# Two-part up products 512 columns wide in the last two feed-forwards, and unread identity products at three changes of stage

## The chip, the cores and the metric

The kernel runs on one core of one Trainium2 chip. The metric is the device time of one execution in microseconds, as the median of several runs. All data is float32.

## The reference, cut to what matters

Four residual layers work on 256 tokens of 1024 channels. Each has a token mixer (pooling in layers 0 and 3, stick-breaking attention in layer 1, a state-space layer in layer 2), a cross-attention to 256 memory tokens, and a gated feed-forward of 2816 channels. The feed-forward is what the change touches:

```python
def conv_glu_ffn(h, w_up, conv_w, conv_b, w_down):
    u = h @ w_up                                   # (256, 1024) @ (1024, 2 * 2816)
    u = sum(conv_w[CONV_WIDTH - 1 - k] * causal_shift(u, k) for k in range(CONV_WIDTH)) + conv_b
    val, gate = jnp.split(u, 2, axis=-1)
    return (jax.nn.silu(gate) * val) @ w_down      # (256, 2816) @ (2816, 1024)

for i in range(DEPTH):
    ...
    h = h + f          # f = conv_glu_ffn(rms_norm(h, ffn_norm_g[i]), ...)
return rms_norm(h, final_norm_g)
```

## The kernel before, in words

**Products in three parts.** Every operand of a large product is split into a rounded part (`hi`, type fp32r, a cast on ScalarE, line 70) and the rest (`lo`, a subtraction on VectorE, line 71). A product x·w is then three products on TensorE, which `mm3` issues (lines 65, 66, 67): hi·hi, the weights' hi with the activations' lo, and the weights' lo with the activations' hi. The product of the two rests is left out. Weights come from DRAM by the SP queue (line 88) into `raw` (three buffers), and are split in two halves into `whi` and `wlo` (six buffers in `wp`, three in the pool `fp` of the down projection).

**Norm and turn.** `norm_T` (line 200) is at the head of the attention mixer (`"mix"`), of the cross-attention (`"xa"`) and of the feed-forward (`"ffn"`). Token block 0 is normed, turned by TensorE against the identity (`turned`, line 223, eight transposes of 128x128) and split into `hi` and `lo` (`taken`); then block 1. `self.fill(...)` places work of other stages in between, such as parts of the next layer's K and V products. In the feed-forward of layer 0 that is the start of the state-space layer's preparation (`s5_start`), in those of layers 1 and 2 a part of a K product, in that of layer 3 nothing.

**The feed-forward.** `ffn` (line 1225) goes through 22 chunks `fc` of 128 channels, two to a load of weights (`f2`). A chunk has a value half (s = 0) and a gate half (s = 1). Each half sums eight pieces `c` of 128 input channels, of 256 token columns: 24 products a half, 48 a chunk, in one PSUM bank `u` of 512 columns. Behind them come, for each half, the convolution's middle tap and bias on ScalarE (line 1259) and its two other taps on VectorE (line 1261), both reading PSUM; then the SiLU (line 1263), the product of both halves (line 1264) and the split into `gg`. The down products (`flush`, 12 of 512 columns, into four banks `acc` that are kept through the stage) are issued two chunks later, through the list `pend`. At the end of the stage the last two chunks' down products follow, and `add_residual` adds the banks to `h` and sums the squares for the next norm (line 157).

**PSUM and order.** Four banks rotate for all products of the pool `psm`, four more are the `acc` banks. The order of instructions on each engine is made by a scheduler from the order of the code and the readiness that it expects; each engine then works in that order. `behind(...)` holds work back by hand.

Of the kernel before, what the change touches and what calls it, by code (L numbers as in the profile page):

```python
# [8 lines left out]
F32 = mybir.dt.float32  # L9
# [5 lines left out]
P = 128  # L15
T = 256
TT = T // P
D = 1024
DC = D // P
# [17 lines left out]
class Trunk:  # L37
# [152 lines left out]
    def norm_natural(self):  # L190
# [2 lines left out]
            self.normed(self.h, tt, xs[:, tt, :], self.ss[tt])  # L193
        return xs

    def transposed(self, xs, c, ps):
        for tt in range(TT):
            self.nc.tensor.transpose(ps[:, tt * P : (tt + 1) * P], xs[:, tt, c * P : (c + 1) * P], self.ident[:])

    def norm_T(self, which, l, where, scaled=True):  # L200

        nc = self.nc
        xs = self.big.tile([P, TT, D], F32, tag="xs", name="xs")
        g = xs[:, 1, :]
        nc.sync.dma_start(g, self.a[which + "_norm_g"][l].partition_broadcast(P))
        hi, lo = self.act_pair()
        self.fill(where + "0")
        halves = [slice(0, 512), slice(512, D)]

        def gained(tt):  # L210

            for s in halves:
                x = nc.vector.tensor_mul(xs[:, tt, s], self.h[:, tt, s], g[:, s])
            return x.ins

        def turned(tt):

            both = []
            for c4 in range(2):
                ps = self.bank() if tt else self.psa.tile([P, 512], F32, tag=f"acc{c4}", name="tp")  # L220
                for j in range(4):
                    c = 4 * c4 + j
                    nc.tensor.transpose(ps[:, j * P : (j + 1) * P], xs[:, tt, c * P : (c + 1) * P], self.ident[:])
                both.append(ps)
            return both

        def taken(tt, both):
            for c4 in range(2):
                f = lambda t: t[:, 4 * c4 : 4 * c4 + 4, tt * P : (tt + 1) * P]
                self.last = self.split(f(hi), f(lo), both[c4][:].rearrange("p (c t) -> p c t", c=4))  # L230

        if scaled:
            self.normed(self.h, 0, xs[:, 0, :], self.ss[0], g)
        else:
            gained(0)
        both = turned(0)

        if scaled:
            r = self.rstd(self.ss[1])
            first = self.squared, self.scaled  # L240
        else:
            first = gained(1),
        with self.behind(*first):
            taken(0, both)
        self.fill(where)
        if scaled:
            gained(1)
            nc.vector.tensor_scalar_mul(xs[:, 1, halves[0]], xs[:, 1, halves[0]], r[:, 0:1])
            nc.scalar.mul(xs[:, 1, halves[1]], xs[:, 1, halves[1]], r[:, 0:1])
        both = turned(1)  # L250
        self.fill(where + "1")
        taken(1, both)
        self.after = [(), self.last, self.last]
        self.transposed_all = (*self.last, self.powed)
        return hi, lo
# [968 lines left out]

    def ffn(self, l, fp):
        nc = self.nc
        hi, lo = self.norm_T("ffn", l, "fnorm")
        up = self.a["ffn_w_up"][l].rearrange("(c p) (s n) -> p c s n", p=P, s=2)
        down = self.a["ffn_w_down"][l].rearrange("(c p) n -> p c n", p=P)
        accs = self.accs()  # L1230
        pend = []

        ug = self.acts.tile([P, 8, T], F32, tag="ah", name="ug")
        gg = self.acts.tile([P, 8, T], F32R, tag="al", name="gg")

        def flush():
            fc, gh, gl, w, k = pend.pop(0)
            for tt in range(TT):
                s = slice(tt * P, (tt + 1) * P)
                for nh in range(2):  # L1240
                    self.mm3(accs[2 * nh + tt][:], (gh[:, s], gl[:, s]), w(k, slice(512 * nh, 512 * (nh + 1))), fc == 0, fc == FC - 1)

        for f2 in range(FC // 2):
            wu = [self.load(up[:, :, s, T * f2 : T * (f2 + 1)], DC, T) for s in range(2)]
            wd = self.load(down[:, 2 * f2 : 2 * f2 + 2, :], 2, D, fp)
            for j in range(2):
                fc = 2 * f2 + j
                self.fill(f"up{fc}")
                ps = self.bank("u")
                u = ug[:, 2 * (fc % 3) : 2 * (fc % 3) + 2, :]  # L1250
                for s in range(2):
                    out = ps[:, s * T : (s + 1) * T]
                    for c in range(DC):
                        self.mm3(out, wu[s](c, slice(j * P, (j + 1) * P)), (hi[:, c, :], lo[:, c, :]), c == 0, c == DC - 1)
                for s in (1, 0):
                    out = ps[:, s * T : (s + 1) * T]
                    col = s * FC + fc
                    cw = [self.cwT[:, l, k, col : col + 1] for k in range(4)]
                    nc.scalar.activation(u[:, s, :], out, AF.Identity, bias=cw[3], scale=cw[2])  # L1259
                    for sh in (1, 2):  # L1260
                        nc.vector.scalar_tensor_tensor(u[:, s, sh:], out[:, : T - sh], cw[2 - sh], u[:, s, sh:], ALU.mult, ALU.add)  # L1261
                g = ug[:, 6 + fc % 2, :]
                nc.scalar.activation(g, u[:, 1, :], AF.Silu)
                nc.vector.tensor_mul(g, g, u[:, 0, :])
                gh, gl = gg[:, 2 * (fc % 4), :], gg[:, 2 * (fc % 4) + 1, :]
                last = self.split(gh, gl, g)
                pend.append((fc, gh, gl, wd, j))
                if len(pend) > 2:
                    flush()

        self.after = [(), last, last]
        while pend:
            flush()
        for nh in range(2):
            for tt in range(TT):
                self.add_residual(nh, tt, accs[2 * nh + tt])
# [145 lines left out]
```

## Time and profile before

| | us |
|---|---|
| median of 3 runs | 1481.85 |
| lowest, highest | 1478.66, 1484.84 |
| profiled execution, its time | 1482.43 |
| profiled execution, span from the first to the last instruction | 1480.7 |
| TensorE busy in the span | 1426.4 |
| VectorE busy | 1096.5 |
| ScalarE busy | 839.3 |
| mean granted TensorE clock, share of full speed | 0.982 |

Times in rows of the trace count from the span's start. The up products of a feed-forward are the rows `u<-ah,whi`, `u<-al,whi` and `u<-ah,wlo`; the down products are `acc<-whi,gg` and `acc<-wlo,gg`; the transposes of `norm_T` are `tp<-ident,xs` for token block 0 and `mm<-ident,xs` for block 1. Engines are PE (TensorE), PEld (its weight loads), DVE (VectorE), ACT (ScalarE), POOL (GpSimd) and SP. In a row of the order in time, the first column is the start in us, the second the length, and brackets hold the idle time before it and what ended it. In a sum over a stretch stand the stretch and its length, then for each engine the busy time and the number of instructions, then the granted clock, the busy share of the DMA engines and GB/s.

### The profile page before, as it was taken

The numbers are of one execution on the slowest core, as the hardware profiler recorded it, in microseconds if no ns is written. First come the engines' busy times: TensorE is split into PE (matmuls) and PEld (weight loads), VectorE is DVE, ScalarE is ACT, GpSimd is POOL, SyncE is SP. The second block draws the span as 40 slices with busy tenths as digits, with TensorE's granted clock in tenths as the row PEclk, the third lists the DMA queues.
The fourth block names the chain that finished last, engine by engine and source line by source line (L and its number), as shares of the span: only waits on it lengthen the run. The fifth ranks groups of instructions, "written<-read, shape, count | busy, mean of one in ns | idle before, by whom it ended". The sixth has DMA issues, their size and how long they took to land.

```text
span 1480.7 us, 25386 instructions
## 1 busy us (share of the span) xinstructions
PE 1426.4 (96%) x10354; PEld 1316.4 (89%) x10354; DVE 1096.5 (74%) x1722; ACT 839.3 (57%) x1351; POOL 124.3 (8%) x128
## 2 busy tenths in 40 slices
PE   7999999998999999999997789999999999999997
PEld 7897999998998989999987668999999999899996
DVE  6969888767886577978783857678677776677675
ACT  7654655547895455645453256565555565565553
POOL 3401000000000000111103500000000030000000
PEclk9999999999999999999998989999999999999999
DMA  7667656645444545776758675455555563465551
GB/s 261 229 164 220 222 199 206 219 135 166 151 149 161 187 148 191 250 225 221 235 192 234 238 233 170 158 171 199 183 187 182 178 210 136 143 220 171 189 181 43
DMA packets 205681, 279.74 MB, mean 189 GB/s; under 512 B 23740, under 2 KB 163132, under 8 KB 203644
## 3 DMA queue, kind: packets, MB, share of 16 engines
q1 hardware_dynamic: 198556, 260.46, 53.0%
q0 software_dynamic: 6432, 17.13, 3.5%
q8 instruction: 81, 1.33, 0.4%
q10 hardware_dynamic: 576, 0.52, 0.1%
q14 instruction: 36, 0.29, 0.1%
HBM read 264.24 MB, written 16.94 MB: 190 GB/s over the span
## 4 chain that ended last, share of the span: by engine, by line
PE 79%; DVE 9%; DMA 6%; ACT 3%; issue 1%; POOL 0%; SPq 0%; DVEq 0%; POOLq 0%; ACTq 0%
PE u L66 10%; PE u L67 10%; PE u L65 10%; PE mm L66 7%; PE mm L65 7%; PE mm L67 7%; PE acc L65 7%; PE acc L66 7%; PE acc L67 7%; DMA raw<-in_ffn_w_up_dram 3%; DVE wlo L71 2%; DMA raw<-in_xa_wkv_dram 2%; ACT whi L70 1%; DVE ug L1261 1%; DMA raw<-in_s_w_glu_dram 1%
## 5 line engine op out<-in xcount | busy, mean ns | idle before, releaser
L71 DVE TENSOR_TENSOR wlo<-raw,whi 128x1024 fp32r<-128x1024 f32 x430 | 519.3, 1220 | 157.0 <-ACT whi L70 148.4
L70 ACT CAST whi<-raw 128x1024 fp32r<-128x1024 f32 (+1 forms) x450 | 460.1, 1045 | 198.8 <-DMA raw<-in_ffn_w_up_dram 55.3
L65 PE MATMUL u<-ah,whi 128*128 128x256 f32 x1408 | 400.6, 285 | 1.7 <-DVE ug L1261 1.3
L66 PE MATMUL u<-al,whi 128*128 128x256 f32 x1408 | 399.8, 284 | 0.4 <-DVE al L71 0.4
L67 PE MATMUL u<-ah,wlo 128*128 128x256 f32 x1408 | 399.5, 284 | 0.0
L65 PEld LDWEIGHTS u<-ah,whi 128*128 128x128 f32 x1408 | 271.2, 193 | 6.3 <-issue 2.5
L66 PEld LDWEIGHTS u<-al,whi 128*128 128x128 f32 x1408 | 271.2, 193 | 3.4 <-DVE al L71 0.9
L67 PEld LDWEIGHTS u<-ah,wlo 128*128 128x128 f32 x1408 | 271.2, 193 | 0.0
L1261 DVE SCALAR_TENSOR_TENSOR ug<-u,cwT,ug 128x255 f32<-128x255 f32 x352 | 168.5, 480 | 101.3 <-ACT ug L1259 96.2
L1259 ACT ACTIVATE ug<-u,cwT 128x256 f32<-128x256 f32 x176 | 99.0, 563 | 185.6 <-PE u L67 125.0
L65 PE MATMUL acc<-whi,gg 128*128 128x512 f32 x352 | 138.0, 392 | 0.0
L66 PE MATMUL acc<-wlo,gg 128*128 128x512 f32 x352 | 137.9, 392 | 0.0
L67 PE MATMUL acc<-whi,gg 128*128 128x512 f32 x352 | 136.9, 389 | 0.0
L66 PE MATMUL mm<-al,whi 128*128 128x256 f32 x384 | 109.9, 286 | 0.1
L65 PE MATMUL mm<-ah,whi 128*128 128x256 f32 x384 | 109.8, 286 | 0.0
L67 PE MATMUL mm<-ah,wlo 128*128 128x256 f32 x384 | 109.4, 285 | 0.0
L176 POOL TENSOR_TENSOR r<-v,mhalf 128x1 f32<-128x1 f32 x28 | 22.7, 813 | 810.5 <-DVE v L172 678.7
L67 PEld LDWEIGHTS acc<-whi,gg 128*128 128x128 f32 x352 | 66.1, 188 | 14.4
L65 PEld LDWEIGHTS acc<-whi,gg 128*128 128x128 f32 x352 | 66.4, 189 | 11.7
L66 PEld LDWEIGHTS acc<-wlo,gg 128*128 128x128 f32 x352 | 66.4, 189 | 10.7
L66 PEld LDWEIGHTS mm<-al,whi 128*128 128x128 f32 x384 | 74.6, 194 | 0.8 <-DVE al L71 0.6
L65 PEld LDWEIGHTS mm<-ah,whi 128*128 128x128 f32 x384 | 74.6, 194 | 0.3 <-ACT ah L70 0.2
(355 smaller groups left out, 2564.9 us busy)
## 6 DMA issues: line engine op xcount, KB each, us to landing
raw<-in_ffn_w_up_dram SPq DMA_DIRECT2D x88, 1024.0 KB
raw<-in_ffn_w_down_dram SPq DMA_DIRECT2D x44, 1024.0 KB
raw<-in_xa_wkv_dram SPq DMA_DIRECT2D x30, 1024.0 KB
raw<-in_xa_wq_dram SPq DMA_DIRECT2D x16, 1024.0 KB
raw<-in_xa_wo_dram SPq DMA_DIRECT2D x16, 1024.0 KB
raw<-in_sb_w_qkv_dram SPq DMA_DIRECT2D x12, 1024.0 KB
raw<-in_s_w_glu_dram SPq DMA_DIRECT2D x8, 1024.0 KB
raw<-in_sb_w_o_dram SPq DMA_DIRECT2D x4, 1024.0 KB
```

What stands on the lines that cost most here:

```text
L65: mm(out, lh, rh, start=start, stop=False)
L66: mm(out, lh, rl, start=False, stop=False)
L67: self.multiplied = mm(out, ll, rh, start=False, stop=stop).ins
L70: x = self.nc.scalar.copy(hi, src)
L71: y = (eng or self.nc.vector).tensor_sub(lo, src, hi.bitcast(F32))
L176: self.powed = nc.gpsimd.tensor_tensor(r[:], v[:], self.mhalf[:], ALU.pow).ins
L1259: nc.scalar.activation(u[:, s, :], out, AF.Identity, bias=cw[3], scale=cw[2])
L1261: nc.vector.scalar_tensor_tensor(u[:, s, sh:], out[:, : T - sh], cw[2 - sh], u[:, s, sh:], ALU.mult, ALU.add)
```

## The change

In the feed-forwards of layers 2 and 3 (`wide`), the activations' two parts lie side by side: four pieces in one tile, four in the other, each piece 256 columns of `hi` and then 256 of `lo`. The weights' hi part multiplies all 512 columns in one product; the weights' lo part multiplies the 256 columns of `hi`, into the right half of the same bank. A half of a chunk then fills one bank, a chunk two. The two columns' halves of a bank are put together by a copy on ScalarE and an addition on VectorE, into `sums` in SBUF, and the convolution's steps read that instead of PSUM, the value half first instead of the gate half.

Apart from that, `turn_over` issues products of the identity with itself (full precision, 256 columns) into a bank that nothing reads: six before the first transposes of layer 1's attention, and five behind the first transposes of the feed-forwards of layers 0 and 3.

```diff
+    def turn_over(self, n):
+        ps = self.bank("idle")
+        for _ in range(n):
+            self.nc.tensor.matmul(ps[:, :T], self.ident[:], self.ident[:].unsqueeze(1).to_broadcast([P, 2, P]), start=True, stop=True)
...
-    def norm_T(self, which, l, where, scaled=True):
+    def norm_T(self, which, l, where, scaled=True, wide=False):
...
-        hi, lo = self.act_pair()
+        if wide:
+            hi, lo = self.act_pair(4, 2 * T)
+        else:
+            hi, lo = self.act_pair()
...
         def taken(tt, both):
             for c4 in range(2):
                 f = lambda t: t[:, 4 * c4 : 4 * c4 + 4, tt * P : (tt + 1) * P]
-                self.last = self.split(f(hi), f(lo), both[c4][:].rearrange("p (c t) -> p c t", c=4))
+                to = [(hi, lo)[c4][:, :, n + tt * P : n + (tt + 1) * P] for n in (0, T)] if wide else (f(hi), f(lo))
+                self.last = self.split(*to, both[c4][:].rearrange("p (c t) -> p c t", c=4))
...
+        if (l, which) == (1, "mix"):
+            self.turn_over(6)
         both = turned(0)
+        if (l, which) in ((0, "ffn"), (3, "ffn")):
+            self.turn_over(5)
...
     def ffn(self, l, fp):
-        hi, lo = self.norm_T("ffn", l, "fnorm")
+        wide = l > 1
+        hi, lo = self.norm_T("ffn", l, "fnorm", wide=wide)
...
+        sums = self.kv.tile([P, 2, 2, T], F32, tag="vh", name="sums") if wide else None
+
+        def up_wide(out, w, j):
+            for c in range(DC):
+                x = (hi, lo)[c // 4][:, c % 4, :]
+                wh, wl = w(c, slice(j * P, (j + 1) * P))
+                nc.tensor.matmul(out, wh, x, start=c == 0, stop=False, skip_group_check=True)
+                nc.tensor.matmul(out[:, T:], wl, x[:, 0:T], start=False, stop=c == DC - 1, skip_group_check=True)
...
-                ps = self.bank("u")
...
+                if wide:
+                    both = [self.bank("u"), self.bank("u")]
+                    for s in range(2):
+                        up_wide(both[s][:], wu[s], j)
+                else:
+                    ps = self.bank("u")
...
-                for s in (1, 0):
-                    out = ps[:, s * T : (s + 1) * T]
+                for s in range(2) if wide else (1, 0):
+                    if wide:
+                        out = sums[:, fc % 2, s, :]
+                        nc.scalar.copy(out, both[s][:, T:])
+                        nc.vector.tensor_add(out, out, both[s][:, 0:T])
+                    else:
+                        out = ps[:, s * T : (s + 1) * T]
```

More of the change, by code (lines that the diff above doesn't have):

```diff
@@ L1248, in ffn @@
                 self.fill(f"up{fc}")
-                ps = self.bank("u")
                 u = ug[:, 2 * (fc % 3) : 2 * (fc % 3) + 2, :]
-                for s in range(2):
-                    out = ps[:, s * T : (s + 1) * T]
-                    for c in range(DC):
-                        self.mm3(out, wu[s](c, slice(j * P, (j + 1) * P)), (hi[:, c, :], lo[:, c, :]), c == 0, c == DC - 1)
-                for s in (1, 0):
-                    out = ps[:, s * T : (s + 1) * T]
+                if wide:
[4 more added lines that the diff above has]
+                    ps = self.bank("u")
+                    for s in range(2):
+                        out = ps[:, s * T : (s + 1) * T]
+                        for c in range(DC):
+                            self.mm3(out, wu[s](c, slice(j * P, (j + 1) * P)), (hi[:, c, :], lo[:, c, :]), c == 0, c == DC - 1)
+                for s in range(2) if wide else (1, 0):
[4 more added lines that the diff above has]
+                    else:
+                        out = ps[:, s * T : (s + 1) * T]
                     col = s * FC + fc
```

## The prediction, made before the kernel was run

> **What bounds the kernel now.** I read the page first: busy shares, the clock row, the chain.
>
> ```profile
> PE 1426.4 (96%) x10354; PEld 1316.4 (89%) x10354; DVE 1096.5 (74%) x1722; ACT 839.3 (57%) x1351; POOL 124.3 (8%) x128
> ...
> PEclk9999999999999999999998989999999999999999
> ...
> PE 79%; DVE 9%; DMA 6%; ACT 3%; issue 1%; POOL 0%; SPq 0%; DVEq 0%; POOLq 0%; ACTq 0%
> ```
>
> TensorE carries the time: busy 96% of the span, 79% of the chain. VectorE, at 74%, is next. Since a busy TensorE need not be a fast one, I went to the sums over stretches: layer 3's feed-forward, and in it one pass of 17.00 us (two of the 22 chunks).
>
> ```profile
> core 0: us, PE busy (x) PEld busy (x) DVE busy (x) ACT busy (x) POOL busy (x), PEclk, DMA share, GB/s
> 1284.00:1472.00 188.00, 188.00 (x1317) 176.97 (x1316) 134.01 (x200) 104.51 (x156) 0.00 (x0) 0.99 0.49 166
> 1360.02:1377.02 17.00, 17.00 (x122) 16.02 (x121) 12.27 (x19) 9.55 (x14) 0.00 (x0) 1.00 0.55 187
> ```
>
> TensorE has no idle time there, at full clock, while VectorE has 4.73 us of 17.00 free, ScalarE 7.45, and the DMA engines work 0.55 of the time. A chunk takes 8.50 us. The order in time on TensorE says what it is made of (first column is the start):
>
> ```profile
> 1304.98 0.28 PE L65 MATMUL u<-ah,whi 128*128 128x256 f32 x1
> ...
> 1310.62 0.28 PE L67 MATMUL u<-ah,wlo 128*128 128x256 f32 x1
> 1310.73 0.40 PE L65 MATMUL acc<-whi,gg 128*128 128x512 f32 x1
> ...
> 1313.26 0.39 PE L67 MATMUL acc<-whi,gg 128*128 128x512 f32 x1
> 1313.48 0.28 PE L65 MATMUL u<-ah,whi 128*128 128x256 f32 x1
> ```
>
> From 1304.98 to 1310.73 stand the 48 up products of a chunk (2 halves, 8 pieces, 3 products): 5.75 us, 0.120 apart. From 1310.73 to 1313.48 stand 12 down products of 512 columns: 2.75 us, 0.229 apart. The durations in the rows (0.28, 0.40) overlap, so I reckon with distances. Two products of 256 columns take 0.240, one of 512 takes 0.229: some 0.011 us goes with the product, not with its columns.
>
> **The change part by part.** *Wide products.* For each of 2 layers x 22 chunks x 2 halves x 8 pieces = 704 places, three products of 256 columns (0.360) become one of 512 and one of 256 (0.229 + 0.120 = 0.349). TensorE is the bound throughout these stages, so all of it is on the path: 704 x 0.011 = 7.7 us. Bounds: none (0) if the short product behind the long one costs more than in a row of its own kind, and 704 x 0.020 = 14 us with the last long product's 0.22 (1313.26 to 1313.48) for all of them. I take 8.0, near the mean of 12 and a little towards that shorter one. Weight loads fall from three to two a place and lie beside the products as before.
>
> The Trainium skill, "TensorE: Matmul & The Clock Gate", section "Wait — 56ns, not 53.3ns?", puts a warm product's fixed part at some 2.5 ns; by that the sum would be 704 x 2.5 ns = 1.8 us instead of 8.0. The rows above differ, and the measurement decides.
>
> *The conversions behind it.* Per half ScalarE copies 256 columns out of PSUM and VectorE adds 256. Nearest rows of 256 columns:
>
> ```profile
> L71 DVE TENSOR_TENSOR gg<-ug,gg 128x256 fp32r<-128x256 f32 x88 | 36.8, 418 | 4.0 <-ACT gg L70 3.8
> L1263 ACT ACTIVATE ug<-ug 128x256 f32<-128x256 f32 x88 | 35.8, 407 | 0.0
> L70 ACT CAST gg<-ug 128x256 fp32r<-128x256 f32 x88 | 35.7, 406 | 51.4 <-DVE ug L1264 51.3
> ```
>
> VectorE's chunk grows from 12.27 / 2 = 6.14 by 2 x 0.42 to 6.97 us, ScalarE's from 4.78 by 2 x 0.41 to 5.59; a chunk of TensorE shrinks from 8.50 to 8.50 - 16 x 0.0114 = 8.32. So VectorE is at 84%, and I cost this at nothing. Cover: a chunk's down products are issued only after the up products of the chunk two later (the list `pend`), some 14 us. Where the cover is shortest is the last chunk: its down products come 24 products (5.5 us) behind its up products, and its conversions now run like this:
>
> ```profile
> 1463.94 0.56 ACT L1259 ACTIVATE ug<-u,cwT 128x256 f32<-128x256 f32 x1 [4.30 <-PE u L67]
> 1464.53 1.00 DVE L1261 SCALAR_TENSOR_TENSOR ug<-u,cwT,ug 128x255 f32<-128x255 f32 x2 [3.71 <-ACT ug L1259]
> ...
> 1468.17 0.42 DVE L71 TENSOR_TENSOR gg<-ug,gg 128x256 fp32r<-128x256 f32 x1 [0.47 <-ACT gg L70]
> ```
>
> That is 4.65 us from 1463.94 to 1468.59. With two banks, the value half is complete 2.8 us earlier and its steps no longer stand in this row; the gate half keeps copy, add, activation with its hand-over (0.59), two steps (1.00) and the gate's four of about 0.45: 4.3 us. Still inside 5.5. The chunk uses two of four banks instead of one; the next but one needs them again 14 us later, hidden likewise. The sums lie in the place of the cross-attention's V, which the next layer takes again long after; no DMA is added or moved. In the queues of ScalarE and VectorE the conversions of the next weights stand behind the new steps, and TensorE waits for those. If that cover goes, every us of VectorE over 8.32 in a chunk shows 44 times.
>
> *The first product of the stage.* It now needs both parts of its piece, not only the cast one. Layer 3's change of stage on TensorE:
>
> ```profile
> 1278.38 1.03 PE L223 MATMUL tp<-ident,xs 128*128 128x128 f32 x8
> 1281.58 1.06 PE L223 MATMUL mm<-ident,xs 128*128 128x128 f32 x8 [2.17 <-issue]
> 1282.88 0.51 PE L65 MATMUL u<-ah,whi 128*128 128x256 f32 x2 [0.24 <-ACT ah L70]
> 1283.61 0.39 PE L66 MATMUL u<-al,whi 128*128 128x256 f32 x1 [0.22 <-DVE al L71]
> ```
>
> Only the product at 1282.88 ran before VectorE's part was there at 1283.6; to lose that head start costs 0.12 to 0.2 in each of two layers: +0.3 in all.
>
> *Identity products.* A drop of the clock is read from TensorE's work in equal steps of 3.41 us and the clock in the next one:
>
> ```profile
> 140.44:143.85 3.41, 3.19 (x13) 2.90 (x14) 3.41 (x5) 3.41 (x5) 0.00 (x0) 0.50 0.74 267
> 335.00:338.41 3.41, 1.06 (x8) 0.86 (x8) 2.95 (x6) 2.79 (x11) 1.29 (x2) 1.00 0.09 13
> 338.41:341.83 3.42, 3.16 (x12) 2.58 (x13) 2.63 (x5) 2.71 (x5) 0.00 (x0) 0.50 0.84 292
> 341.83:345.24 3.41, 3.41 (x18) 3.41 (x17) 1.74 (x3) 3.40 (x4) 0.00 (x0) 0.50 0.04 11
> 809.45:812.87 3.42, 2.12 (x24) 1.73 (x16) 2.57 (x5) 1.84 (x5) 3.42 (x5) 1.00 0.74 260
> 812.87:816.28 3.41, 3.37 (x15) 2.80 (x16) 2.83 (x4) 3.38 (x4) 3.39 (x5) 1.00 0.90 322
> 1280.49:1283.91 3.42, 1.87 (x12) 1.46 (x13) 2.73 (x5) 2.88 (x5) 0.46 (x1) 1.00 0.00 0
> 1283.91:1287.32 3.41, 3.41 (x18) 3.41 (x17) 3.26 (x4) 3.41 (x5) 0.00 (x0) 0.50 0.00 0
> ```
>
> 1.06 and 1.87 us of work were followed by half clock, 2.12 was not. A step at half clock holds 18 products at its edges, so some 16 whole ones, 0.213 each; at 0.120 they take 1.92, so a full step at full clock is worth 1.49 us.
>
> What does one identity product cost? It is of full-precision operands; the nearest row with such operands and no transposing is
>
> ```profile
> 844.53 1.95 PE L1080 MATMUL acc<-tu,v 128*32 128x128 f32 x64
> ```
>
> By the code these are 32 products in four column groups, two records each. If the groups run side by side, 16 records follow each other at 0.12 for 128 columns; so 0.23 for 256, and 0.46 for a product's two. If not, 0.03 each, 0.12 for a product. I take 0.46, since it fills the wait: five are 2.3 us, six 2.8.
>
> Layer 3: five start at 1279.4 and end at 1281.7, where the next transposes start at 1281.58: delay 0.1. The step 1280.49 then holds 1.87 + 1.2 us, above 2.12: clock kept, -1.5 + 0.1 = -1.4. Bounds 0 and -1.9 (half of 3.7 us). Layer 0: the half-clock step holds 13 products, at most 13 x 0.093 = 1.2 us; I take -1.0, since some waits are in it; bounds 0 and -1.2. They also push the state-space transposes behind them back on TensorE and with them ScalarE's copies; covered by products that need the second half of the pieces only later. Layer 1's attention:
>
> ```profile
> 336.89 1.06 PE L223 MATMUL tp<-ident,xs 128*128 128x128 f32 x8 [3.02 <-DVE v L172]
> 338.52 1.97 PE L223 MATMUL mm<-ident,xs 128*128 128x128 f32 x8 [0.57 <-DVE xs L248]
> 340.31 0.58 PE L65 MATMUL mm<-ah,whi 128*128 128x256 f32 x1
> 341.04 0.58 PE L66 MATMUL mm<-al,whi 128*128 128x256 f32 x1
> ```
>
> Six fit the wait of 3.02, so the transposes do not slip and step 335.00 holds 1.06 + 1.4. But step 338.41 then holds 1.06 of transposes, two single products and a run from about 340.5 or 341: close to 2.1, undecided. Both steps at full clock: 4.20 us from 341.04 to 345.24 become 2.36, and the transposes' 1.97 become 1.06, of which 0.5 is kept: -2.4. Only the first: about -0.9. And if the order on TensorE puts them into an earlier wait, between the last down products, they cost up to 6 x 0.46 = +2.8. I take -1.2.
>
> *Sum.* -8.0 + 0.3 - 1.4 - 1.0 - 1.2 = -11.3. The profiled execution took 1482.4 (its span 1480.7 and 1.7 around it), 0.6 above the median of 1481.85: 1481.9 - 11.3 = 1470.6, say **1470.5**.
>
> **The rivals.** *A, the forecast*: 1470.5; own range 1466 to 1474.4, from -15.5 (9.5 for the wide part, all three clocks kept with 2.4 + 1.9 + 1.2) to -7.4.
>
> *B, the clocks fall as before or the fillers cost what they bring*: only the wide part stays, 1481.9 - 7.7 = 1474.2, with one delay 1477. For: the step of 3.41 us runs free of the kernel, and a shift of a few us moves the idle time to other steps. Against: 2.12 sufficed. The Trainium skill, same page, "Part 4: PE-mode transpose", says that transposes do not count as work for the clock; by it the three steps would still fall, and the time would be B's. The row 809.45, where 16 of 24 records are transposes and the clock stayed, speaks against it.
>
> *C, slower: VectorE and ScalarE become the bound by handing over.* In order, a half now goes ScalarE, VectorE, ScalarE, VectorE. If no weight conversion stands in the waits of VectorE, a chunk costs it 6.97 + 2 x 0.59 (two activations) + 0.41 (gate) + 0.47 (cast) = 9.0; 44 x (9.0 - 8.50) = +22, less 3.6 of the clocks: 1500. It decides from 8.50 + 3.6 / 44 = 8.6 a chunk. For: 84% busy in order. Against: a pass has 4.73 us free, of which the adds take 1.7, and its conversions of weights can stand in these waits. *C2*, a chunk between 8.4 and 8.5: 1474.4 to 1480.
>
> *D, the pair costs as much as the three*, the fixed part being that of the long one's weight change: only the clocks, 1481.9 - 3.6 + 0.3 = 1478.6.
>
> **How the numbers follow.** A 0.58, B 0.18, C 0.06, C2 0.11, D 0.07. Half a per cent is 7.4 us, about what a measurement here can tell from no change. Faster (under 1474.4): A and half of B, 0.67. Slower (over 1489): C, 0.06. Same: 0.27. Range 1464.5 to 1479: below A's end for steps of the clock that fall elsewhere (one is 1.5 us), up to D, leaving out C and the ends of C2 and A.
>
> **What would show it.** Right: in layers 2 and 3 a chunk of 8.3 us, up products 0.35 a pair, TensorE still without idle time, VectorE near 84%; full clock in the steps after the three changes; 16 identity products of about 0.46 inside the old waits. Wrong: TensorE waiting for `gg` or `wlo` in those layers; pairs at 0.36; identity products between down products; half clock behind them.

## The result, and the profile after

The changed kernel takes 1471.79 us (median of 4 runs, 1471.04 to 1473.01) against 1480.53 for the kernel before beside it (1478.66 to 1484.84): ratio 0.9946, 95% interval 0.9924 to 0.9967, a gain of 8.7 us. The prediction of 1470.5 is 1.3 us below that. The profiled execution of the change took 1471.25, its span 1469.5, 11.2 us less than the span of before.

From the page of the changed kernel, the busy times, the clock in 40 slices and the chain by engine:

```profile
PE 1420.6 (97%) x9682; PEld 1279.3 (87%) x9682; DVE 1122.0 (76%) x1810; ACT 866.2 (59%) x1439; POOL 124.4 (8%) x128
...
PEclk9999999999999999999999999999999999999999
...
PE 75%; DVE 11%; DMA 7%; ACT 3%; issue 2%; POOL 0%; SPq 0%; DVEq 0%; POOLq 0%; ACTq 0%
```

TensorE issues 672 records less (704 fewer in the wide products, 32 more for the 16 identity products), VectorE and ScalarE 88 more each. TensorE is still the bound. The two slices with an 8 in the clock row of before are gone, but they lie in the state-space layer (777 to 814 and 851 to 888 us), where the change has no instruction. Sum over a stretch of the changed kernel inside layer 2's feed-forward (layer 3's is alike):

```profile
1000.00:1140.00 140.00, 140.00 (x738) 119.45 (x737) 114.12 (x188) 90.67 (x154) 0.00 (x0) 1.00 0.56 188
```

No idle time on TensorE, full clock. A chunk takes 8.386 us, and of that VectorE works 114.12 / 140 x 8.386 = 6.84, or 82%. The order in time on TensorE in layer 3:

```profile
1321.07 0.39 PE L1260 MATMUL u<-ah,whi 128*128 128x512 f32 x1
1321.30 0.28 PE L1261 MATMUL u<-ah,wlo 128*128 128x256 f32 x1
1321.41 0.40 PE L1260 MATMUL u<-ah,whi 128*128 128x512 f32 x1
...
1326.71 0.40 PE L65 MATMUL acc<-whi,gg 128*128 128x512 f32 x1
...
1329.46 0.39 PE L1260 MATMUL u<-ah,whi 128*128 128x512 f32 x1
```

Sixteen pairs stand from 1321.07 to 1326.71: 5.64 us, 0.3525 a pair. The down products take 2.75 as before. So a chunk went from 8.50 to 8.39, where 8.32 was expected.

The changes of stage, in the order of time on TensorE of the changed kernel (layer 0, layer 1's attention, layer 3):

```profile
135.92 2.32 PE L200 MATMUL idle<-ident 128*128 128x256 f32 x10
...
333.24 2.75 PE L200 MATMUL idle<-ident 128*128 128x256 f32 x12
336.42 1.06 PE L233 MATMUL tp<-ident,xs 128*128 128x128 f32 x8 [0.43 <-DVE v L172]
338.05 1.43 PE L233 MATMUL mm<-ident,xs 128*128 128x128 f32 x8 [0.57 <-DVE xs L263]
...
1270.88 1.03 PE L233 MATMUL tp<-ident,xs 128*128 128x128 f32 x8
1271.75 2.32 PE L200 MATMUL idle<-ident 128*128 128x256 f32 x10
1274.09 1.06 PE L233 MATMUL mm<-ident,xs 128*128 128x128 f32 x8
1276.11 0.50 PE L1260 MATMUL u<-ah,whi 128*128 128x512 f32 x1 [0.96 <-DVE ah L71]
```

Five identity products take 2.32, six 2.75: 0.46 each. They stand in the waits of before; what is left of layer 1's wait is 0.43 of 3.02, and layer 3's second transposes follow the first by 3.21, before by 3.20. The clock behind them, as sums over stretches of the length of a clock step:

```profile
141.00:144.41 3.41, 2.90 (x22) 2.69 (x23) 3.41 (x5) 3.41 (x5) 0.18 (x1) 1.00 0.77 293
339.38:342.79 3.41, 3.07 (x24) 2.87 (x24) 1.65 (x3) 3.24 (x4) 0.00 (x0) 1.00 0.52 179
1276.11:1279.52 3.41, 3.41 (x19) 2.99 (x20) 3.27 (x4) 3.41 (x5) 0.00 (x0) 1.00 0.03 5
```

All three at full clock, where before all three places showed 0.50.

The starts of the same instructions in both traces, after minus before, give the account of the two profiled executions (a chunk's term in the prediction is 8.0 / 44 = 0.18):

| place | change in time, us | predicted |
|---|---|---|
| start-up | +0.6 | - |
| layer 0's feed-forward, head | -1.1 | -1.0 |
| layer 1's attention | -2.3 | -1.2 |
| layer 1's feed-forward and the state-space layer, to 889.00 of before | -2.2 | - |
| layer 2's feed-forward, head and first three chunks | -0.3 | -0.4 |
| layer 2's next 18 chunks | -2.0 | -3.3 |
| from there to layer 3's first transposes, one chunk with it | -0.1 | -0.2 |
| layer 3's feed-forward, head and first three chunks | -1.6 | -1.8 |
| layer 3's next 18 chunks | -2.0 | -3.3 |
| end, one chunk with it | -0.1 | -0.2 |

What the head of layer 3 costs and gains can be taken apart with the kernel that has the identity products alone (in the experiments below). From the second transposes to the first up product behind the first down products it has the rows 1276.70 and 1298.60, the changed kernel 1274.09 and 1295.91:

```profile
1276.70 1.06 PE L233 MATMUL mm<-ident,xs 128*128 128x128 f32 x8
...
1298.60 0.28 PE L65 MATMUL u<-ah,whi 128*128 128x256 f32 x1
```

```profile
1295.91 0.39 PE L1260 MATMUL u<-ah,whi 128*128 128x512 f32 x1
```

Before it is 23.40 us (1281.58 to 1304.98), with the identity products alone 21.90, with the whole change 21.82. So the clock gives 1.5 there. The wide products give 0.08 more, three chunks of 0.113 less 0.26 for the later start.

The -2.2 ahead of layer 2 was in no term. In the trace of before two steps there ran at half clock; the same work in the changed kernel ran at full clock. That gave 2.75; a step at half clock late in layer 1's feed-forward (759.22) and other waits took 0.5 back. First before, then after:

```profile
874.30:877.72 3.42, 2.52 (x6) 2.04 (x7) 3.31 (x4) 2.98 (x3) 0.00 (x0) 0.50 0.66 235
877.72:881.13 3.41, 3.41 (x9) 2.64 (x9) 0.00 (x0) 0.00 (x0) 0.00 (x0) 0.50 0.73 161
```

```profile
869.50:883.99 14.49, 13.04 (x61) 10.59 (x60) 8.73 (x9) 9.39 (x10) 0.00 (x0) 1.00 0.63 206
```

The change has no instruction there, and where the waits of this stretch fall among the steps differs between traces: the kernel with the wide products alone, with the same order of instructions up to here, is 5.9 us behind before's trace at 797.78 and 0.5 behind it at 883.10. Without this stretch and the start-up, the places that the change touches gave 9.5 of the 11.2 us; the medians differ by 8.7.

### The profile page after: what moved, and what is told of

Same layout as the page of the kernel before. It is cut to its first block, busy times and chain, and to the rows that moved or that the text cites. A ratio compares the mean times of both kernels' runs of the same rounds, so it can differ in the third digit from the quotient of the medians.

```text
span 1469.5 us, 24256 instructions
## 1 busy us (share of the span) xinstructions
PE 1420.6 (97%) x9682; PEld 1279.3 (87%) x9682; DVE 1122.0 (76%) x1810; ACT 866.2 (59%) x1439; POOL 124.4 (8%) x128
## 4 chain that ended last, share of the span: by engine, by line
PE 75%; DVE 11%; DMA 7%; ACT 3%; issue 2%; POOL 0%; SPq 0%; DVEq 0%; POOLq 0%; ACTq 0%
PE u L1260 11%; PE mm L66 7%; PE mm L65 7%; PE mm L67 7%; PE acc L65 7%; PE acc L66 7%; PE acc L67 7%; PE u L1261 6%; PE u L66 4%; PE u L65 4%; PE u L67 4%; DMA raw<-in_ffn_w_up_dram 3%; DVE wlo L71 3%; DMA raw<-in_xa_wkv_dram 2%; ACT whi L70 2%
## 5 line engine op out<-in xcount | busy, mean ns | idle before, releaser
L65 PE MATMUL u<-ah,whi 128*128 128x256 f32 x704 | 200.9, 286 | 2.4 <-DVE ug L1298 2.0
L66 PE MATMUL u<-al,whi 128*128 128x256 f32 x704 | 199.9, 284 | 0.5 <-DVE al L71 0.5
L67 PE MATMUL u<-ah,wlo 128*128 128x256 f32 x704 | 199.8, 284 | 0.0
L65 PEld LDWEIGHTS u<-ah,whi 128*128 128x128 f32 x704 | 135.6, 193 | 5.3 <-issue 3.4
L66 PEld LDWEIGHTS u<-al,whi 128*128 128x128 f32 x704 | 135.7, 193 | 1.7 <-DVE al L71 0.7
L67 PEld LDWEIGHTS u<-ah,wlo 128*128 128x128 f32 x704 | 135.7, 193 | 0.0
L1260 PE MATMUL u<-ah,whi 128*128 128x512 f32 x352 | 128.3, 398 | 1.0 <-DVE ah L71 1.0
L1260 PE MATMUL u<-al,whi 128*128 128x512 f32 x352 | 128.2, 398 | 0.0
L1298 DVE SCALAR_TENSOR_TENSOR ug<-sums,cwT,ug 128x255 f32<-128x255 f32 (+1 forms) x176 | 84.4, 481 | 37.4 <-ACT ug L1296 35.3
L1261 PE MATMUL u<-ah,wlo 128*128 128x256 f32 x352 | 98.9, 281 | 0.0
L1261 PE MATMUL u<-al,wlo 128*128 128x256 f32 x352 | 98.7, 281 | 0.0
```

The source lines that it names most:

```text
L65: mm(out, lh, rh, start=start, stop=False)
L66: mm(out, lh, rl, start=False, stop=False)
L67: self.multiplied = mm(out, ll, rh, start=False, stop=stop).ins
L1260: nc.tensor.matmul(out, wh, x, start=c == 0, stop=False, skip_group_check=True)
L1261: nc.tensor.matmul(out[:, T:], wl, x[:, 0:T], start=False, stop=c == DC - 1, skip_group_check=True)
```

## The experiments

Ratios are to the kernel before, run beside each; its medians there were 1481.28, 1480.51 and 1480.73, single runs between 1475 and 1487.

**Each half of the change alone.**

```diff
-        if (l, which) == (1, "mix"):
-            self.turn_over(6)
-        if (l, which) in ((0, "ffn"), (3, "ffn")):
-            self.turn_over(5)
```

> The change without its identity products. Theory 1 (the parts add up, each by its own rows): the wide products alone give 44 chunks x 0.114 us = 5.0 us, less 0.6 at the two stage heads, so a ratio to before of about 0.997; chunks of 8.39 us in layers 2 and 3; half clock returns in the steps after the change of stage in layer 0's feed-forward, layer 1's attention and layer 3's feed-forward. Rival (the clock was kept by something else, the earlier start of work): no half clock there and a ratio of 0.9945 as with the whole change.

Without identity products: 1480.03 us, ratio 0.999 (0.9975 to 1.0004). The three places are at half clock again, sums over stretches:

```profile
143.56:146.97 3.41, 3.41 (x18) 3.41 (x18) 3.41 (x4) 3.41 (x5) 0.00 (x0) 0.50 0.40 143
...
341.53:344.94 3.41, 2.97 (x14) 2.40 (x13) 2.16 (x4) 2.66 (x5) 0.00 (x0) 0.50 0.70 243
...
1280.20:1283.61 3.41, 2.76 (x11) 2.07 (x10) 2.91 (x4) 3.18 (x5) 0.00 (x0) 0.50 0.00 0
```

From the same product in layer 2 to the end, first before and then this kernel:

```profile
889.00:1480.70 591.70, 578.75 (x3976) 538.57 (x3974) 419.77 (x630) 331.55 (x517) 20.02 (x16) 0.99 0.51 170
```

```profile
889.49:1477.20 587.71, 574.53 (x3272) 501.39 (x3270) 446.35 (x718) 359.33 (x605) 19.44 (x16) 0.99 0.52 171
```

That is 4.0 less: 5.0 for 44 chunks at 8.386, less 0.3 for the later start in layer 3 and 0.7 for the clock there. The change of stage in layer 3 has two steps at half clock in this trace (1280.20 to 1287.02), as in the grouped kernel without identity products below, where before has one.

The runs' median shows only 1.3 of the 4.0. Ahead of layer 2's feed-forward the order on every engine is that of before, so no wait of the edit lies there. What the runs show of the rest is the clock: the mean granted clock of these 12 runs has a median of 0.982, that of the 20 runs of the kernel before beside them 0.984. Among those 20, a run with 0.001 less clock took some 1.5 us more (a straight line through them), so 0.002 are worth some 3 us. That is an estimate; why the clock of these runs was lower is not shown beyond the one step in layer 3.

```diff
-        wide = l > 1
+        wide = False
```

> The change without the wide products. Theory 1: the identity products alone give 1.1 + 2.3 + 1.5 = 4.9 us, ratio about 0.9967, chunks of 8.50 us. Rival (each drop of the clock only moves to another wait of the state-space layer): ratio 0.999 to 1.001, with as many half-clock steps as before in all.

Identity products alone: 1476.06, 0.9971 (0.9951 to 0.999), full clock at all three places, chunks of 8.50. The mean granted clock of its trace is 0.989 against 0.982 before, so the drops did not only move. Together the two halves give 1.3 + 5.2 = 6.5, where the change's runs give 8.7; the intervals are wider than the difference.

**Order of the products.** All eight long products of a half, then its eight short ones:

```diff
             for c in range(DC):
...
                 nc.tensor.matmul(out, wh, x, start=c == 0, stop=False, skip_group_check=True)
+            for c in range(DC):
...
                 nc.tensor.matmul(out[:, T:], wl, x[:, 0:T], start=False, stop=c == DC - 1, skip_group_check=True)
```

> The whole change, but within a half first the eight products of 512 columns and then the eight of 256. Theory 1 (a pair costs 0.353 instead of 0.347 because long and short alternate; long ones come at 233 to 241 ns behind a short one, 227 in a row of their own kind): a half takes 8 x 0.227 + 8 x 0.120 = 2.78 us instead of 2.82, a chunk 8.30 to 8.35 instead of 8.39, 1.5 to 3.5 us in all, ratio to before 0.992 to 0.9935. Rival (the cost goes with the long product's columns or with PSUM, whatever stands ahead): a chunk stays at 8.39, ratio 0.9945.

1469.17 (1468.16 to 1470.84), 0.9916 (0.990 to 0.9931). Order in time on TensorE:

```profile
1311.00 1.07 PE L1259 MATMUL u<-ah,whi 128*128 128x512 f32 x4
1311.91 1.07 PE L1259 MATMUL u<-al,whi 128*128 128x512 f32 x4
1312.82 0.64 PE L1262 MATMUL u<-ah,wlo 128*128 128x256 f32 x4
1313.29 0.64 PE L1262 MATMUL u<-al,wlo 128*128 128x256 f32 x4
1313.77 1.09 PE L1259 MATMUL u<-ah,whi 128*128 128x512 f32 x4
1314.70 1.07 PE L1259 MATMUL u<-al,whi 128*128 128x512 f32 x4
...
1316.56 0.40 PE L65 MATMUL acc<-whi,gg 128*128 128x512 f32 x1
```

(`ah` and `al` are here the tiles of pieces 0 to 3 and 4 to 7, so eight long ones stand from 1311.00 to 1312.82.) Four long ones take 0.91 behind long ones, the down products among them, and 0.93 behind short ones; four short ones take 0.47 to 0.48. The up products take 5.56, a chunk 8.306, and 8.386 - 8.306 = 0.08 less than in pairs. Only the order differs, so the rival falls. One new wait comes at the end of layer 2:

```profile
1161.32 0.50 PE L65 MATMUL acc<-whi,gg 128*128 128x512 f32 x1 [0.95 <-ACT gg L70]
```

The last chunk's conversions now end later than the products that covered them.

The value half in long, short order and the gate half in short, long order saves two changes of width a chunk, one of them from short to long (the edit against the grouped order):

```diff
-    up_wide(both[s][:], wu[s], j)
+    up_wide(both[s][:], wu[s], j, 1 - s)   # last argument 0 (s = 1): the short products first
```

> The grouped order, but the gate half takes its short products first, so long ones stand next to the down products and short ones next to each other. Theory 1 (what costs is each change from short to long, five products slowed by 0.028 us in all): one change a chunk less, 44 x 0.028 = 1.2 us less than grouped, a chunk of 8.28 us instead of 8.31. Rival (the slow products belong to the change of bank, not of length): a chunk stays at 8.31.

A chunk takes 8.286, 0.02 less of the 0.028 forecast, 0.9 us in all, so most of the slowing goes with the change of length. The time, 1469.74, 0.9923 (0.9896 to 0.9951), is not to be told from the grouped order's.

**The clock.** Each identity product becomes four 128x128 transposes of the identity:

```diff
-            self.nc.tensor.matmul(ps[:, :T], self.ident[:], ...)
+        for _ in range(4 * n):
+            self.nc.tensor.transpose(ps[:, :P], self.ident[:], self.ident[:])
```

> The whole change, with each identity product replaced by four 128x128 transposes of the identity (20 or 24 in a row, some 0.109 us each, so as long as before). Theory 1 (what counts for the clock is that TensorE is busy): full clock behind the three changes of stage as with products, time as with the change. Rival (transposes do not count as work for the clock, the rule of the Trainium skill, TensorE: Matmul & The Clock Gate, Part 4): half clock returns in the three places, some 4.9 us more than the change.

1473.38, 0.9946 (0.9925 to 0.9968), the ratio of the change. Sums over stretches behind the three places:

```profile
141.35:144.76 3.41, 2.90 (x22) 2.70 (x23) 3.41 (x5) 3.41 (x5) 0.18 (x1) 1.00 0.77 300
339.74:343.15 3.41, 3.07 (x24) 2.87 (x24) 1.66 (x3) 3.24 (x4) 0.00 (x0) 1.00 0.52 180
1278.29:1281.70 3.41, 3.41 (x19) 2.99 (x20) 3.26 (x4) 3.41 (x5) 0.00 (x0) 1.00 0.00 0
```

Transposes keep the clock as products do. By the Trainium skill, "TensorE: Matmul & The Clock Gate", "Part 4: PE-mode transpose", they would not count; these rows say otherwise, and they count here.

Only two identity products at each place, on the grouped order, and none, on the same:

```diff
-            self.turn_over(6)   # 5 at the two others
+            self.turn_over(2)   # e10: removed
```

> The grouped order with two identity products at each of the three places instead of six and five: 0.93 us of work each. Theory 1 (what counts is how much of a step of 3.41 us TensorE works, with its bound between 1.9 and 2.1 us): half clock is back at layer 1's attention, where the wait of 3.0 us is left open by 2.1, and at one or both of the other two, 2 to 5 us more than grouped. Rival (a short burst inside the wait is enough to restart the count of idle time): full clock at all three, time as grouped.

> The grouped order without any identity product. Theory 1 (the parts add up): the wide products alone give 44 x 0.19 = 8.4 us less 1.6 at heads and ends, ratio to before about 0.9955, and what the identity products give is the rest to the grouped order's 0.9916, 5 us or so. Rival (wide products alone give little, as the run with alternating ones and no identity products measured 0.999): 0.998 or more.

Two: 1472.62, 0.9945 (0.9926 to 0.9963), 3.5 us over the grouped kernel's median. None: 1474.37, 0.9955 (0.9938 to 0.9971), 5.2 us over it. The medians are of runs made at different times; by the intervals the kernel without any is slower than the grouped one, and the one with two probably is. With two, each place has one step at half clock again:

```profile
141.83:145.25 3.42, 3.30 (x15) 3.31 (x16) 3.42 (x5) 3.42 (x5) 0.00 (x0) 0.50 0.58 178
339.81:343.22 3.41, 3.30 (x15) 2.66 (x14) 2.15 (x4) 2.77 (x4) 0.00 (x0) 0.50 0.77 266
1275.06:1278.47 3.41, 3.03 (x7) 2.46 (x8) 3.27 (x5) 3.41 (x5) 0.00 (x0) 0.50 0.00 0
```

So the number matters at these places, not only that the wait is broken. Two are 0.93 us of work, five 2.3. At the three places a step ahead of a drop held 1.06 to 1.87 us of work in these traces, and with five or six identity products, or the transposes, none held under 1.97. But this is no sharp bound: in the trace of before itself, a step of the state-space layer held 1.73 us and the next one, from 860.65, ran at 1.00:

```profile
857.24:860.65 3.41, 1.73 (x7) 1.04 (x6) 3.41 (x5) 3.41 (x4) 0.00 (x0) 1.00 0.96 348
```

and in the kernel with more additions, below, a step of 2.90 us (1180.09) was followed by one at 0.50. What else decides is not shown.

More of them, on the grouped order, in the state-space layer, where the clock also falls:

```diff
+        self.turn_over(8)       # before the transposes of ur
...
+        self.turn_over(4)       # after t0 = turn(0, y0)
```

> The grouped order with identity products in two more waits, both in layer 2's state-space mixer: eight before the transposes of the unrolled input, four behind the first transposes of the GLU's input. Theory 1 (a drop of the clock costs what TensorE has to do in it): the clock stays up there (two of five drops of layer 2 less) and 1.5 to 3 us are saved, ratio to before about 0.990. Rival (that stretch waits for transfers and VectorE's scan, so TensorE's clock is worth little there): ratio 0.9916, as grouped.

1473.86, 0.9957 (0.9937 to 0.9977), where the grouped kernel without them has 0.9916 (0.990 to 0.9931): slower by 4.7 us in the medians. The clock did not stay up: it was full through the first new identity products, but from the end of layer 1's feed-forward to layer 2's first up product it has a mean of 0.95 in both traces, with the drops in other places. Order in time in this trace and then in that of the grouped kernel:

```profile
816.78 8.75 DVE L1066 COPY X<-SX 128x256 f32<-128x256 f32 x1 [0.98 <-ACT SX L1046]
...
838.36 0.79 PE L65 MATMUL mm<-whi,mgh 128*128 128x512 f32 x1 [8.95 <-DVE vl L71]
```

```profile
812.96 1.26 DVE L1065 COPY X<-SX 128x256 f32<-128x256 f32 x1 [1.03 <-ACT SX L1045]
...
830.61 0.80 PE L65 MATMUL mm<-whi,mgh 128*128 128x512 f32 x1 [2.45 <-DVE vl L71]
```

The copy with which VectorE begins the scan takes 8.75 us instead of 1.26, and TensorE waits 8.95 for VectorE instead of 2.45. TensorE also waits 5.29 instead of 2.26 for a copy of `v` that stands behind two casts on ScalarE, in both kernels. The order on VectorE, ScalarE and GpSimd is the same in both up to there, so the scheduler moved none of this. Why the copy took so long is not shown, and this trace is of the slowest of the 12 runs (1480.28, the fastest 1468.47): what the median of them lost stays open.

**VectorE as the next bound.** One more subtraction and addition of 256 columns a half, 44 x 4 in all (the sum is taken off and added again):

```diff
                         nc.vector.tensor_add(out, out, both[s][:, 0:T])
+                        nc.vector.tensor_sub(out, out, both[s][:, 0:T])
+                        nc.vector.tensor_add(out, out, both[s][:, 0:T])
```

> The whole change, with the sum of a bank's halves added, subtracted and added again, so two more VectorE operations of 0.41 us per half. Theory 1 (VectorE is hidden as long as its work and its waits for ScalarE fit into TensorE's 8.39 us a chunk): VectorE's work rises from 7.3 to 8.9 us a chunk, over 8.39, so a chunk takes 9 us or more in layers 2 and 3, TensorE shows idle time there, and the kernel is 27 us or more slower than with the change. Rival (there is still room, since ScalarE's waits overlap): chunks stay under 8.6, under 10 us slower.

```profile
1000.00:1140.00 140.00, 140.00 (x738) 119.19 (x737) 134.54 (x259) 92.66 (x155) 0.00 (x0) 1.00 0.59 196
```

A single run: 1473.72, its span 1472.0. VectorE is busy 96%, 8.06 us of a chunk of 8.39, and TensorE has no idle time, here and from the first up product to the last down product of both stages. The theory that had this kernel slower by tens of us had put VectorE's chunk too high, at 8.9. So VectorE is not the bound in these stages, and waits inside its queue are not on the path. The slack shrinks: in layer 2's chunks 9 to 18 the parts of `gg` are ready 8.2 to 10.3 us ahead of their first down product with the change and 5.8 to 7.0 here, and in the first chunks of both stages the scheduler has put some down products between up products.

**Wide products in more layers.** Grouped order in all four, with the sums of layers 0 and 1 in slots of `ug`; then the same without layer 1:

```diff
-        wide = l > 1
+        wide = True     # e9: l != 1
...
-                        out = sums[:, fc % 2, s, :]
+                        out = sums[:, fc % 2, s, :] if l > 1 else ug[:, 4 + s, :]   # e9: the same
```

> The grouped order (eight long, then eight short products) in all four feed-forwards; in layers 0 and 1 the sums lie in two slots of ug, with the convolution's tiles double instead of triple buffered. Theory 1 (TensorE is the bound there too): 44 more chunks x 0.19 us = 8.4 us less than the grouped order of two layers, ratio to before 0.986. Rival (in layers 0 and 1 VectorE has the state-space preparation besides, 155 and 163 us busy of 194 and 195; 37 us of sums go on top, so VectorE or the single buffer becomes the bound): no gain or slower, ratio 0.99 to 1.01, with TensorE idle before products of layers 0 and 1.

> The grouped order in the feed-forwards of layers 0, 2 and 3; layer 1's, where the run with all four showed TensorE waiting, has the three products of before. Theory 1: layer 0's gain stays (3 us by the trace with all four) and layer 1's waits go, ratio to before 0.988 to 0.990. Rival (what layer 0 gains is given back at its end and in the state-space layer's waits): as grouped, 0.9916.

All four: 1468.01 (1464.72 to 1471.99), 0.9915 (0.9888 to 0.9942). Without layer 1: 1469.56, 0.9918 (0.9895 to 0.9941). Both as the grouped kernel, as the rivals forecast. By the starts of the same instructions, layer 0 of the kernel with all four gained 4.5 us on the grouped kernel over its chunks and gave 1.6 back at its end. Layer 1 gained nothing: 197.24 us from its first up to its last down product, 196.75 in the grouped kernel. The order on TensorE of the kernel with all four shows the waits; this is one of the two longest:

```profile
667.64 1.21 PE L1259 MATMUL u<-ah,whi 128*128 128x512 f32 x4 [2.14 <-DVE ug L1292]
```

The sum over most of that stage:

```profile
600.00:740.00 140.00, 134.31 (x905) 112.79 (x903) 126.28 (x210) 82.89 (x150) 21.79 (x24) 1.00 0.72 232
```

Line 1292 is VectorE's addition, the last reader of a PSUM bank of up products: the product waits until a bank is free. VectorE has 126.28 of 140 us there, with the state-space layer's preparation in its queue, and TensorE is idle for 5.7. That VectorE is too busy is not shown by this: with 134.54 of 140 in layer 2 it made no wait. And the wait is not one of wide products alone. In the kernel without layer 1, where that layer has the three products and the triple buffers of before, its feed-forward takes 201.03 us, and the longest wait in it is

```profile
672.41 0.35 PE L65 MATMUL u<-ah,whi 128*128 128x256 f32 x1 [3.60 <-DVE ug L1299]
```

with VectorE itself idle for 5.58 before that, until 667.60, for a weight's cast. Which of the queue's order and the weights' transfers makes these waits was not tried apart. No kernel here is faster than the grouped one by its interval, 0.9916 (0.990 to 0.9931); it is ahead of before, and of the changed kernel (0.9924 to 0.9967) but for a narrow overlap.

## Why the prediction was right, and where not

- **The time was near, partly by luck.** The sum said 11.3 less; the runs gave 8.7 less, and the places that the change touches 9.5 in the traces. The time came out only 1.3 off because the sum starts from 1481.9, and the kernel before measured 1480.53 beside the changed one. In the sum itself two errors go against each other: the wide products gave 3.0 less than forecast, layer 1's attention 1.1 more.
- **Wide products: right mechanism, size off.** The term of 8.0 was 5.0 (0.113 x 44). The step that failed is the distance of 0.349 a pair, put together from products in rows of their own kind; and 8.0 was taken above its own 7.7, towards a bound of 14 that rests on one product's 0.22. Alternating, a pair takes 0.3525. In the grouped order it takes 5.56 / 16 = 0.3475 (0.229 and 0.119), and the chunk's 8.306 is under the predicted 8.32: that experiment shows the loss to be the alternation.
- **VectorE hidden: right.** 6.84 us a chunk measured, 6.97 predicted; TensorE idle nowhere in the chunks of layers 2 and 3, and still nowhere with VectorE at 96%. Rivals C and C2 fall.
- **The last chunk's conversions: right in layer 3, 0.4 short in layer 2.** Order in time of the changed kernel, ScalarE and VectorE, layer 2 and then layer 3:

```profile
1157.40 1.00 DVE L1298 SCALAR_TENSOR_TENSOR ug<-sums,cwT,ug 128x255 f32<-128x255 f32 x2 [0.67 <-ACT ug L1296]
1157.59 0.37 ACT L1290 COPY sums<-u 128x256 f32<-128x256 f32 x1 [0.22 <-PE u L1261]
1158.31 0.41 DVE L1291 TENSOR_TENSOR sums<-sums,u 128x256 f32<-128x256 f32 x1
...
1161.84 0.42 DVE L71 TENSOR_TENSOR gg<-ug,gg 128x256 fp32r<-128x256 f32 x1 [0.47 <-ACT gg L70]
```

```profile
1452.71 0.37 ACT L1290 COPY sums<-u 128x256 f32<-128x256 f32 x1 [1.37 <-PE u L1261]
...
1456.65 0.42 DVE L71 TENSOR_TENSOR gg<-ug,gg 128x256 fp32r<-128x256 f32 x1 [0.47 <-ACT gg L70]
```

  From the gate half's copy to the end of `gg` it is 4.36 us in layer 3, as forecast (4.3): the value half was done ahead. In layer 2 it is 4.67. There the value half came late itself, behind a weight conversion, and its two steps from 1157.40 to 1158.40 held up the gate's addition. The cover held in both, by 0.6 in layer 2. In the grouped order it did not there, and 0.95 showed.
- **First product of the stage: right in sum.** Layer 3's head lost 0.26 (0.12 to 0.2 was forecast): the first long product waits 0.96 for the split of the activations, and the two short products that before ran ahead of it are what is lost. Layer 2's head lost nothing: its first product starts 3.02 us behind the second transposes in both kernels, long after the split. Together that is 0.3, as in the sum.
- **Identity products: sized right, cost as forecast.** 0.46 each, inside the waits, clock kept at all three places. Layer 0 (-1.1 for -1.0) and layer 3 (-1.5 for -1.4) came out as predicted. Layer 1's attention was mis-sized by the choice between its ends: -1.2 was half of -2.4, and both steps stayed at full clock, -2.3. The reading behind it, that 1.87 us of work in a step are too few and 2.12 enough, served at these places but is no rule of these traces, by the step of 1.73 above. Rival B falls, its transposes with the experiment of the transposes.
- **A's lower end** was added up wrongly: 9.5 + 2.4 + 1.9 + 1.2 is 15.0 and not 15.5, and no row is named for the 9.5. The forecast does not rest on it.
- **Rival D** (the pair costs as much as three short ones) falls by 0.3525 against 0.360.

Open stays why the granted clock of the runs with the wide half alone was lower, and how much of a single run's 1475 to 1487 is due to clock steps that fall differently.

## What to carry to other kernels

Price a product by the distance between starts in the mix in which it will be issued, and keep products of one width together: long ones first, then short ones, took 0.08 us off a chunk here, 3.5 us in all, of which a new wait of 0.95 took some back. Before a change of stage, fill the wait with enough work to keep the clock (five or six products did, two did not), and measure it: in the state-space layer more of them gave nothing. Reckon a gain against a median measured beside it, since a base that is 1.3 us off can hide an error of the sum. An engine at 96% can still be hidden where its results are due chunks later; at the last chunk of a stage that slack is nearly gone, and its conversions must be reckoned one by one.

## What was not expected of the hardware

Products of 512 and 256 columns in turn do not cost the sum of their prices in rows of their own kind. In the grouped order, after a short product the distances from the first long ones to the next are 0.233, 0.236, 0.228, 0.233 and 0.231 us (means over 15 chunks of layer 3) before they settle at 0.227: a little under 0.03 lost at each change from short to long. The kernel before has the same five distances in its down products. In pairs long and short cost 0.226 to 0.242 and 0.112 to 0.120, 0.3525 together and not 0.3475 as in the grouped order. The cause is not settled: weight loads and columns are the same in both orders.
